# A two-level Strassen matmul with tanh on one core: s3 made first in a tile of its own, the opening's stores moved, two products of chunk 0 made plain, 24 zero matmuls ahead

## The chip, the cores and the metric

The kernel runs on one core of one Trainium2 chip. The metric is the device time of one launch in microseconds (us). The time before is 1428.15 us, the median of three runs (1426.63, 1428.15 and 1431.34). A single profiled execution of the same kernel took 1431.41 us; its span in the trace is 1429.1 us.

## The reference

```python
m, k, n = 4096, 4096, 4096
# a: [4096, 4096] fp32, b: [4096, 4096] fp32, bias: [4096] fp32
return np.tanh(np.matmul(a, b) + bias)
```

Inputs and output are fp32 in DRAM. The kernel casts a and b to fp16 while loading them, multiplies in fp16 and adds in fp32.

## The kernel before

**Two levels of Strassen.** A straight matmul would need 8192 steps of 128x128 by 128x512 on TensorE (PE). The kernel uses the Winograd form of Strassen's algorithm instead. A *pair* is 256 rows of a; its four quarters are a11, a12 (the first 128 rows, low and high half of k) and a21, a22 (the other 128 rows). VectorE (DVE) forms

- s1 = a21 + a22, s3 = a11 - a21, s2 = s1 - a11, s4 = a12 - s2 from a,
- t1 to t4 in the same way from b,

and seven products of half size take the place of eight: P1 (a11), P2 (a12), P3 (s4), P4 (a22), P5 (s1), P6 (s2), P7 (s3), each against a quarter of b or a t. A *duo* is two pairs. Over a duo most products are *fine*: a second level of the same scheme is laid over the two pairs, so that one product becomes 7 groups of 8 matmuls of 128x256, from sums of the operands of the two pairs (xs3, ys3, zs3 from the two s3's, for instance). A *plain* product takes the two pairs separately, as 2 x 16 matmuls of 128x512. Fine products are `fine_product` (L852) and, in the middle part of the program, L1590; plain ones are `product` (L836).

**Stages.** The columns of b are cut into four chunks of 1024. There are 16 pairs, so 8 duos. The trace shows:

- 0 to about 95 us, the *opening*: 18 matmuls on a tile of zeros (`WARM`, L20, issued at L1986), then the first rows of a come in through transposes on PE (tile `first`, L2106) and through DVE's stream transposes (tile `land`, L510), into tiles o00 to o71; some rows are multiplied with b directly (L2067).
- about 95 to 401 us, the rest of chunk 0, duo by duo (L836, L852). While PE works on one duo, GpSimd (POOL) loads the rows of the next one into `nat` tiles (L534, four DMAs of 128 KB each, cast to fp16), DVE transposes them (L510) and makes the sums (L477).
- about 401 to 1075 us, chunks 1 and 2 together, all fine at 128x512 (L1590).
- about 1075 to 1429 us, chunk 3, all fine at 128x256: pass one (P1, P2, P6 of all duos) and pass two (P7, P5, P4, P3 of all duos, from about 1230 us).

**What sets the order.** The program records each step as an operation with its reads and writes; a planner then simulates engines and DMA (with the constants `RATES`, `SHARES`, `WARM_TIME`, `NAT_LEAD`, `SLACK_OPEN`) and writes down one fixed order for each engine, and one of 51 places in SBUF for each tile. SyncE (SP) issues every store and every load from scratch memory in DRAM, in that order; POOL issues the loads of a and b. ScalarE (ACT) copies to and from PSUM (L480) and does the tanh.

**Names the change touches.** `natural` (L559) loads and sums one pair: with `own=True` (first duo after the opening only) s3 gets a tile of its own first and s1 too; otherwise s1 gets the tile of its own, and s3 is written over a21 once s1 has read a21. `over=True` (the middle duos) leaves s2 to later (`natural_late`), where s2 is written over a11. The opening's two pairs, 0 and 1, do the same with `half_sum` (L2206 to L2208). `keep` stores sums in scratch memory (L598) for the later chunks; `KEEP_AT` says for each of the two opening pairs whether its stores come with its sums (0) or later (1). `STEEP` counts, for each duo of chunk 0 behind the opening's, how many of its products are fine: the first x of P1, P7, P5 (L2282); the others are plain. `TOGETHER` says how many of a chunk's last duos go product by product in place of duo by duo. `BEHIND` is the number of P1's that stand ahead of the first P2 in a pass, `AFTER` a position in the same order.

Of the kernel before, what the change touches and what calls it, by code (L numbers as in the profile page):

```python
# [16 lines left out]
TB = 4  # L17
TP = T // 2
G = 2
WARM = 18  # L20
fp32 = mybir.dt.float32
fp16 = mybir.dt.float16
pair32 = mybir.dt.uint32
ADD = mybir.AluOpType.add
SUB = mybir.AluOpType.subtract
# [9 lines left out]
LASTING = ((), (), (), ())  # L35
SHARED = True
SOFT = 1.5
BEHIND = 2
FARTHER = (50, 65, 40, 50)
THREE = (False, True, True, True)  # L40
AFTER = (6, 6, 6, 7)
HOLD = (1, 1, 1, 3)
KEEP_AT = (0, 1)
NAT_LEAD = 2.0
FIRST = (0, 1)
CLASSIC = 16
LATE_STORES = 2
SLACK_OPEN = 0.8
WHOLE = ()
SPARE = ("a11", "a12", "a22")  # L50
AHEAD = ((), (), (), (), (), ())
# [6 lines left out]
RING = 8  # L58
SPEED, SLACK = 1.0, 0.8
RATES = (  # L60
    {"POOL": (378e3, 3.7), "LONG": (419e3, 3.7), "in": (354e3, 4.1), "out": (377e3, 3.9)},
    {"POOL": (386e3, 3.6), "LONG": (399e3, 3.6), "in": (376e3, 3.4), "out": (380e3, 3.6)},
    {"POOL": (375e3, 3.9), "LONG": (403e3, 3.9), "in": (396e3, 3.4), "out": (395e3, 3.5)},
)
SHARES = (
    ((0.29, 0.49, 0.37), (0.40, 0.53, 0.57)),
    ((0.39, 0.45, 0.47), (0.44, 0.55, 0.58)),
    ((0.32, 0.40, 0.45), (0.47, 0.55, 0.54)),
)
FIRST_AT = 1.4  # L70
WARM_TIME = 6.7
RISE = ((), (4, 4, 4, 4, 4, 4, 4, 4), (4, 4, 4, 4, 4, 4, 4, 4), (4, 4, 4, 4, 4, 4, 4, 4))
SECONDS = (0, 8, 8, 8)
STEEP = ((0, 1, 2, 2, 2, 3), (), ())
BASIS = ("a11", "a12", "a22", "s2")
STORED = BASIS + ("s1", "s3", "s4")
LEFT = ('P6', 'P7', 'P5', 'P4', 'P3')
Q_ORDER = (0, 2, 1, 3)
WIDE = 1
WIDE_LASTING = ('s3', 's1')  # L80
TOGETHER = (0, 0, 0, 0)
WIDE_ORDER = (7, 6, 1, 5, 4, 3, 2, 0)
WIDE_PASSES = ((("P1", 0),), (("P2", 0),), (("P6", 0), ("P7", 1)), (("P4", 0),), (("P5", 0), ("P3", 1)))
TURN = 5
WIDE_EARLY = {'P1': (11.0, 80), 'P2': (11.0, 90), 'P6': (11.0, 100), 'P7': (8.0, 120), 'P4': (11.0, 70), 'P5': (11.0, 50), 'P3': (18.0, 100)}


class Buf:
# [324 lines left out]
def kernel(  # L413
# [142 lines left out]

                add("DVE", turn_time(1024), emit, (tl,), (s[name],), soft=soft)

    def natural(pair, kept, own=False, spare=(), over=False):  # L559
        s = {}  # L560
        for r in range(2):
            natural_rows(pair, r, s)
        if own:
            asum(s, "s3", "a11", "a21", SUB)
        asum(s, "s1", "a21", "a22", ADD)
        if over:
            if kept:
                keep(pair, s, BASIS[:2], spare=spare, soft=3.0)
            asum(s, "s3", "a11", "a21", SUB, over="a21")
            return s  # L570
        asum(s, "s2", "s1", "a11", SUB)
        if not own:
            asum(s, "s3", "a11", "a21", SUB, over="a21")
        if kept:
            keep(pair, s, spare=spare)
        return s
# [25 lines left out]
    def keep(pair, s, names=BASIS, spare=(), after=None, soft=None):  # L602

        for name in names:
            soft = soft or (3.0 if names is BASIS else 12.0)
            if pair % 2 == 0:
                move(name, pair // 2, 1, s[name], 0, 2, True, soft=soft, after=after)
                continue
            move(name, pair // 2, 3, s[name], 1, 1, True, soft=soft, after=after)
            if name not in spare:  # L610
                move(name, pair // 2, 4, s[name], 0, 1, True, soft=soft, after=after)
# [1350 lines left out]
    early = set(range(4, NP)) | set(FIRST)  # L1962
# [197 lines left out]
    d = first_duo  # L2160
# [8 lines left out]
    behind = None  # L2169
    if LATE_STORES:  # L2170
# [3 lines left out]
        behind = plan.ops[-1]  # L2174
# [12 lines left out]
    def half_sum(s, name, x, y, op, over=None, halves=(0, 1)):  # L2187
        x, y = s[x], s[y]
        if name not in s:
            s[name] = s[over] if over else new(name, [P, T, P], atoms=2)  # L2190

        def atoms(v, h):
            return (h,) if len(v.atoms) == 2 else (2 * h, 2 * h + 1)

        for h in halves:
            key = ALL, ds(h * TP, TP)
            tt(
                at(s[name], *key), at(x, *key), at(y, *key), op, TP * P,
                ((x, atoms(x, h)), (y, atoms(y, h))), ((s[name], atoms(s[name], h)),), wide=False,
            )  # L2200
# [5 lines left out]
    d.a, d.last_sum = [], last_sum  # L2206
    for p in FIRST:
        s = {f"a{r + 1}{h + 1}": aq[2 * p + r, h] for r in range(2) for h in range(2)}  # L2208
        half_sum(s, "s1", "a21", "a22", ADD)
        half_sum(s, "s3", "a11", "a21", SUB, over="a21")  # L2210
        half_sum(s, "s2", "s1", "a11", SUB)
        firsts[p] = s
        d.a.append(s)
        if not KEEP_AT[p]:
            keep(p, s, [n for n in BASIS if n != "a22" or p != LATE_STORES - 1], soft=3.0)
    d.c, d.k, d.bop, d.pairs = 0, k0, bop, list(FIRST)
    d.x, d.next, d.put = 0, STEEP[0][0], ()
    d.parts = d.last = d.stays = False
# [5 lines left out]
    for c in range(NC):  # L2224
        duos = [[2 * i, 2 * i + 1] for i in ORDER[c]]
        if c in (WIDE, WIDE + 1):
            if c == WIDE:
                plan.open = 2
                if before:
                    waiting.append(lambda between, before=before: (before(), between()))  # L2230
                wide_pass(c, held)
                before = held = None
                for s in sets:
                    for bank in s:
                        ring.remove(bank.index // 2)
                        ring.append(bank.index // 2)
                whole.update(p for p in range(NP) if held_names.get(p, set()) >= set(HELD))
            continue
        if c >= TWO:
            plan.open = 2  # L2240
            k = load_bias(c)
            finish_bias(k)
            bop, rights = {}, {}
            for name in ("b11", "b21"):
                for blk in range(4):
                    raw_b(bop, c, name, blk, NEAR)
            rights["P1"] = fine_right(bop, "b11", True, NEAR)
            if SECONDS[c]:
                rights["P2"] = fine_right(bop, "b21", True, NEAR)
            if before:  # L2250
                waiting.append(lambda between, before=before: (before(), between()))

            def rest():
                for blk in range(4):
                    for name in ("b12", "b22"):
                        raw_b(bop, c, name, blk, (NEAR, FARTHER[c]))
                    bsums(bop, blk, (NEAR, FARTHER[c]))

            if THREE[c]:
                rest()  # L2260
                rights["P6"] = fine_right(bop, "t2", True, NEAR)
            on_chip = pass_one(c, k, bop, rights, duos, held)
            if not THREE[c]:
                rest()
            pass_two(c, k, bop, rights, duos[::-1], on_chip)
            before = held = None
            continue
        fines = {}
        for i, pairs in enumerate(duos):
            d = Duo()  # L2270
            d.c, d.k, d.bop, d.pairs = c, k, bop, sorted(pairs)
            d.parts = c > 0 and i == 0
            d.last = d.stays = i == len(duos) - 1 and c < TWO - 1
            d.x = STEEP[c][i]
            d.next = (STEEP[c] + (0,))[i + 1]
            duo = d.pairs[0] // 2
            over = OVER and 0 < i < len(duos) - 1
            d.a = [natural(p, p in early, i == 0, SPARE if p % 2 and duo not in WHOLE else (), over) for p in d.pairs]
            for name in BASIS if i == 0 else () if over else BASIS[1:]:
                sigma(name, duo, d.a)  # L2280
            if d.x and not d.parts:
                for name, r in (("P1", "b11"), ("P7", "t3"), ("P5", "t1"))[:d.x]:  # L2282
                    if name not in fines:
                        fines[name] = fine_right(bop, r)
            d.right = fines
            d.put = AHEAD[i]
            for name in d.put:
                if name != "s4":
                    for s in range(2):
                        put_by(d, name, s)  # L2290
# [55 lines left out]
```

## Time and profile before

| what | value |
|---|---|
| time, median of 3 (all) | 1428.15 us (1426.63, 1428.15, 1431.34) |
| the profiled execution: its own time, its span | 1431.41 us, 1429.1 us |
| PE | 1417.6 us busy (99%), 8386 matmuls |
| DVE | 1090.6 us busy (76%) |
| ACT | 395.6 us busy (28%) |
| POOL | 325.4 us busy (23%) |
| mean granted TensorE clock | 0.998 |
| DMA | 399.19 MB, 279 GB/s on average |

All times are from one profiled execution, and those of a place in the program are counted from the start of its span. "Busy" for PE counts matmuls whose ends are modelled and overlap, so the time of a run of matmuls is best taken from the start of its first to the start of what follows. In a timeline row stand the start, the duration of the group, the engine, the line and the operation, `out<-in`, shape and count; in brackets the idle time ahead of it and what ended it. In a windows row stand the stretch, its length, PE's or DVE's busy time and instructions in it, the granted clock (1.00 is full, 0.50 half), the busy share of the 16 DMA engines and GB/s.

### The profile page before, as it was taken

What the parts mean: (1) busy time and instruction counts of PE and PEld (TensorE: products, weight loads), DVE (VectorE), ACT (ScalarE), POOL (GpSimd) and SP (SyncE); (2) the same over time, 40 slices, a digit from 0 to 9 for tenths busy, and PEclk for the clock granted to TensorE, in tenths of its full rate; (3) what the DMA queues carried; (4) which work ended last, traced back from release to release, by engine and by line L of the source; (5) the groups of instructions that cost most, each with busy time, mean ns of one, the idle gap of its engine ahead of it and who ended that gap; (6) DMA issues with size and microseconds to landing.
All of it is one profiled execution on the core that took longest, in us unless ns stands there. A gap on an engine that the chain in (4) does not pass through costs nothing.

```text
span 1429.1 us, 22558 instructions
## 1 busy us (share of the span) xinstructions
PE 1417.6 (99%) x8386; PEld 820.4 (57%) x8386; DVE 1090.6 (76%) x1617; ACT 395.6 (28%) x752; POOL 325.4 (23%) x613
## 2 busy tenths in 40 slices
PE   8999999999999999999999999999999999999998
PEld 3444555555644444444444444444447888888887
DVE  3679878767985476795568787988797689997876
ACT  3121212222233333311111233233323332243433
POOL 8764432334452331100111130000130400000000
PEclk9999999999999999999999999999999999999999
DMA  9999998899999899997889799999999987788883
GB/s 177 180 224 291 278 293 208 216 250 210 284 274 315 235 272 307 280 375 273 270 283 299 264 309 380 338 362 354 332 333 347 281 246 260 251 295 291 314 291 134
DMA packets 167485, 399.19 MB, mean 279 GB/s; under 512 B 25424, under 2 KB 44368, under 8 KB 167376
## 3 DMA queue, kind: packets, MB, share of 16 engines
q1 hardware_dynamic: 104400, 318.03, 61.4%
q0 software_dynamic: 62976, 79.73, 33.6%
q8 instruction: 66, 1.08, 0.3%
q14 instruction: 43, 0.35, 0.1%
HBM read 327.68 MB, written 149.68 MB: 334 GB/s over the span
## 4 chain that ended last, share of the span: by engine, by line
PE 78%; DMA 1%; DVE 1%; ACT 0%; issue 0%; SPq 0%; DVEq 0%
PE ps L1590 47%; PE ps L852 25%; PE ps L836 6%; DMA xa<-a 1%; DVE parts L477 0%; ACT parts L1388 0%; DVE za L688 0%; DVE s L477 0%; DVE a L477 0%; DVE ps L477 0%; DVE t L477 0%; DVE cs L477 0%; DVE a L510 0%; ACT ps L480 0%; SPq L491 0%
## 5 line engine op out<-in xcount | busy, mean ns | idle before, releaser
L763 POOL DMA_DIRECT2D b<-in_b_dram x320 | 169.8, 535 | 608.9 <-DMA out_dram<-u 165.4
L480 ACT COPY ps<-ps 128x512 f32<-128x512 f32 (+1 forms) x218 | 101.9, 468 | 445.7 <-PE ps L1590 308.9
L534 POOL DMA_DIRECT2D nat<-in_a_dram x224 | 118.5, 533 | 204.7 <-DMA nat<-in_a_dram 47.3
L477 DVE TENSOR_TENSOR parts<-ps,parts 128x256 f32<-128x256 f32 (+1 forms) x131 | 73.8, 564 | 75.0 <-PE ps L1590 39.6
L477 DVE TENSOR_TENSOR u<-ps,u 128x512 f32<-128x512 f32 x160 | 106.1, 685 | 28.2 <-PE ps L1590 27.4
L836 PEld LDWEIGHTS <-a 128*128 128x128 f16 x768 | 75.1, 98 | 86.9 <-DVE a L477 0.2
L477 DVE TENSOR_TENSOR ps<-ps,parts 128x256 f32<-128x256 f32 (+1 forms) x155 | 85.2, 555 | 38.7 <-PE ps L1590 23.0
L480 ACT COPY parts<-ps 128x256 f32<-128x256 f32 (+1 forms) x153 | 70.1, 463 | 135.8 <-DVE ps L477 45.2
L1590 PE MATMUL ps<-b,zs 128*128 128x512 f16 x448 | 105.8, 379 | 0.0
L1590 PEld LDWEIGHTS <-ya 128*128 128x128 f16 x624 | 61.0, 98 | 73.6
L836 PE MATMUL ps<-b,a 128*128 128x512 f16 x448 | 99.1, 379 | 0.0
L510 DVE STREAM_TRANSPOSE a<-nat 128x512 uint32<-128x512 uint32 x112 | 73.1, 689 | 21.1 <-DMA nat<-in_a_dram 15.2
L2067 PE MATMUL ps<-b,o 128*128 128x512 f16 x384 | 84.9, 384 | 0.0
L1590 PEld LDWEIGHTS <-zs 128*128 128x128 f16 x512 | 50.1, 98 | 60.2
L1590 PEld LDWEIGHTS <-xa 128*128 128x128 f16 x512 | 50.1, 98 | 60.2
L477 DVE TENSOR_TENSOR b<-b,b 128x2048 f16<-128x2048 f16 (+2 forms) x76 | 68.2, 909 | 12.6 <-DMA b<-in_b_dram 10.1
L1590 PE MATMUL ps<-b,za 128*128 128x512 f16 x320 | 75.6, 379 | 0.0
L836 PE MATMUL ps<-t,a 128*128 128x512 f16 x320 | 72.3, 379 | 0.0
L498 ACT ACTIVATE parts<-ps 128x512 f32<-128x512 f32 x50 | 29.7, 596 | 145.6 <-PE ps L836 97.2
L2067 PEld LDWEIGHTS <-o 128*128 128x128 f16 x384 | 37.8, 99 | 45.6 <-issue 1.1
L1590 PEld LDWEIGHTS <-za 128*128 128x128 f16 x384 | 37.6, 98 | 45.3
L852 PEld LDWEIGHTS <-ya 128*128 128x128 f16 x592 | 57.9, 98 | 7.1
(177 smaller groups left out, 2586.3 us busy)
## 6 DMA issues: line engine op xcount, KB each, us to landing
b<-in_b_dram POOLq DMA_DIRECT2D x320, 128.0 KB, 7.9
ya<-a SPq DMA_DIRECT2D x70, 512.0 KB, 6.8
xa<-a SPq DMA_DIRECT2D x70, 512.0 KB, 6.7
u<-U SPq DMA_DIRECT2D x62, 512.0 KB, 6.9
nat<-in_a_dram POOLq DMA_DIRECT2D x224, 128.0 KB, 7.8
U<-u SPq DMA_DIRECT2D x48, 512.0 KB, 7.0
ys<-s SPq DMA_DIRECT2D x46, 512.0 KB, 4.9
xs<-s SPq DMA_DIRECT2D x46, 512.0 KB, 5.4
```

Source lines behind the costliest of these rows:

```text
L477: dve(n, lambda: nc.vector.tensor_tensor(out=o(), in0=x(), in1=y(), op=op), reads, writes, wide, **kw)
L480: act(n, lambda: nc.scalar.copy(o(), x()), reads, writes, **kw)
L498: act(NB, lambda: nc.scalar.activation(o[ALL], src[ALL], TANH), (src,), (o,), soft=2.0)
L510: nc.vector.transpose(dst[ALL].rearrange("P t m -> P (t m)").bitcast(pair32).rearrange("P (U m) -> P U m", m=P)[:, ds(t0 // 2, nu), ds(row ...
L534: nc.gpsimd.dma_start(out=tl[(ds(q * QP, QP), *key)], in_=src)
L763: nc.gpsimd.dma_start(out=dst.rearrange("p t j n -> p t (j n)") if j is None else dst, in_=src)
L836: nc.tensor.matmul(bank[ALL], left_tile(left, k + t + shift), rb.tile(t), start=start and k == t0 and t == 0, stop=k + t == t0 + nt - 1, s ...
L852: nc.tensor.matmul(bank[ALL, HALF[half]], left_tile(buf, at_ * TP + i * TB + t), rb.tile(t), start=False, stop=i == 1 and t == TB - 1, ski ...
L1590: nc.tensor.matmul(bank[ALL, cols], left_tile(buf, at_ * TP + i * TB + t), rb.tile(t, half), start=start and not (i or t), stop=i == 1 and ...
L2067: nc.tensor.matmul(bank[ALL], left_tile(left, t), rb.tile(tb), start=start, stop=stop, skip_group_check=True,)
```

## The change

The diff, cut to what has an effect that the prediction speaks of:

```diff
-WARM = 18
+WARM = 24
-BEHIND = 2
+BEHIND = 3
-AFTER = (6, 6, 6, 7)
+AFTER = (6, 6, 6, 5)
-KEEP_AT = (0, 1)
+KEEP_AT = (0, 0)
-NAT_LEAD = 2.0
+NAT_LEAD = 1.0
-SLACK_OPEN = 0.8
+SLACK_OPEN = 1.0
-WARM_TIME = 6.7
+WARM_TIME = 7.6
-STEEP = ((0, 1, 2, 2, 2, 3), (), ())
+STEEP = ((0, 1, 2, 2, 2, 2), (), ())
-TOGETHER = (0, 0, 0, 0)
+TOGETHER = (0, 0, 0, 3)
...
-    def natural(pair, kept, own=False, spare=(), over=False):
+    def natural(pair, kept, spare=(), over=False):
...
-        if own:
-            asum(s, "s3", "a11", "a21", SUB)
-        asum(s, "s1", "a21", "a22", ADD)
+        asum(s, "s3", "a11", "a21", SUB)
+        asum(s, "s1", "a21", "a22", ADD, over="a21")
         if over:
             if kept:
                 keep(pair, s, BASIS[:2], spare=spare, soft=3.0)
-            asum(s, "s3", "a11", "a21", SUB, over="a21")
             return s
         asum(s, "s2", "s1", "a11", SUB)
-        if not own:
-            asum(s, "s3", "a11", "a21", SUB, over="a21")
...
-        half_sum(s, "s1", "a21", "a22", ADD)
-        half_sum(s, "s3", "a11", "a21", SUB, over="a21")
+        half_sum(s, "s3", "a11", "a21", SUB)
+        half_sum(s, "s1", "a21", "a22", ADD, over="a21")
...
-            keep(p, s, [n for n in BASIS if n != "a22" or p != LATE_STORES - 1], soft=3.0)
+            keep(p, s, [n for n in BASIS if n != "a22" or p != LATE_STORES - 1], after=behind, soft=3.0)
```

Besides, numbers of the planner's model of DMA (`RATES`, `SHARES`) and of how early it loads (`FARTHER`, and for chunks 1 and 2 `WIDE_EARLY`) are changed, which moves single steps of DVE, ACT and SP past one another and gives tiles other places in SBUF. By `STEEP`, P5 of the last duo of chunk 0 is fine before and plain after. PE has 8368 matmuls after in place of 8386: six more of zeros, 56 of 128x256 fewer and 32 of 128x512 more. DVE has 15 sums fewer, ACT 10 copies fewer; POOL's and SP's numbers of DMAs stay (608 and 725).

**DVE, the rows ahead of the fourth duo's P7 in chunk 0 (269 to 280 us in the trace before).** The names are tiles; a number behind a name tells one pair's tile from another's. First before:

```order
L510 STREAM_TRANSPOSE a22_2452<-nat_2359 128x2x8x32
L510 STREAM_TRANSPOSE a21_2461<-nat_2359 128x2x8x32
L477 TENSOR_TENSOR s1_2491<-a21_2461,a22_2452 128x2048
L477 TENSOR_TENSOR a21_2461<-a11_2258,a21_2461 128x2048
L477 TENSOR_TENSOR ys3_2504<-a21_2461 128x1024
L510 STREAM_TRANSPOSE a22_2471<-nat_2415 128x2x8x32
L510 STREAM_TRANSPOSE a21_2474<-nat_2415 128x2x8x32
L477 TENSOR_TENSOR s1_2517<-a21_2474,a22_2471 128x2048
L477 TENSOR_TENSOR a21_2474<-a11_2269,a21_2474 128x2048
L477 TENSOR_TENSOR ys3_2504<-ys3_2504,a21_2474 128x1024
```

and after:

```order
L510 STREAM_TRANSPOSE a21_2478<-nat_2385 128x2x8x32
L477 TENSOR_TENSOR s3_2497<-a11_2274,a21_2478 128x2048
L477 TENSOR_TENSOR ys3_2504<-s3_2497 128x1024
L510 STREAM_TRANSPOSE a22_2510<-nat_2342 128x2x8x32
L510 STREAM_TRANSPOSE a21_2481<-nat_2433 128x2x8x32
L477 TENSOR_TENSOR s3_2523<-a11_2296,a21_2481 128x2048
L477 TENSOR_TENSOR ys3_2504<-ys3_2504,s3_2523 128x1024
L477 TENSOR_TENSOR zs3_2535<-s3_2523,s3_2497 128x1024
L477 TENSOR_TENSOR zs3_2535<-s3_2523,ys3_2504 128x1024
L510 STREAM_TRANSPOSE a22_2510<-nat_2433 128x2x8x32
L477 TENSOR_TENSOR a21_2481<-a21_2481,a22_2510 128x2048
```

Before, each pair's s1 stands between the transposes and its s3 (the row `a21 <- a11, a21`); after, s3 stands directly behind the transpose of a21, and the last a22 and s1 (the row `a21 <- a21, a22`) come behind all that P7 needs.

**PE, the last duo of chunk 0, around the start of P5 (about 381 us before).** Before:

```order
L836 LDWEIGHTS s2_3433
L836 MATMUL ps_1_239<-t2_861,s2_3433 128x512
L852 LDWEIGHTS s1_3375
L852 MATMUL ps_6_273<-t1_1111,s1_3375 128x256
L852 LDWEIGHTS s1_3375
```

and after:

```order
L832 LDWEIGHTS s2_3453
L832 MATMUL ps_1_245<-t2_867,s2_3453 128x512
L832 LDWEIGHTS a21_3293
L832 MATMUL ps_4_267<-t1_1154,a21_3293 128x512
L832 LDWEIGHTS a21_3293
```

Behind the last matmul of P6 (s2 against t2) stands P5 (s1 against t1): before in groups of 128x256, after at 128x512 from s1 in a21's place. The plain P5 is 32 matmuls in place of 56.

**SP, its first rows behind the load of the bias (97 to about 131 us before).** a_0_68 to a_0_70 and s_0_71 are the scratch for a11, a12, a22 and s2 of the first duo, out_dram is the output. Before:

```order
L598 DMA a_0_68<-o_224 128x2048
L598 DMA a_0_69<-o_402 128x2048
L598 DMA a_0_70<-o_404 128x2048
L598 DMA s_0_71<-s_760 128x2048
L491 DMA out_dram<-parts 128x512 x2
L598 DMA a_0_70<-o_417 128x1024 x2
L598 DMA a_2_82<-a_1044 128x2048
L491 DMA out_dram<-parts 128x512
L598 DMA a_2_83<-a_1068 128x2048
L491 DMA out_dram<-parts 128x512 x12
```

and after:

```order
L491 DMA out_dram<-parts 128x512
L594 DMA a_0_70<-o_423 128x1024 x2
L491 DMA out_dram<-parts 128x512
L594 DMA a_2_82<-a_1051 128x2048
L491 DMA out_dram<-parts 128x512 x8
L594 DMA a_0_68<-o_230 128x2048
L594 DMA a_0_69<-o_408 128x2048
L594 DMA a_0_70<-o_410 128x2048
L594 DMA a_0_68<-o_255 128x1024 x2
L594 DMA a_0_69<-o_414 128x1024 x2
L491 DMA out_dram<-parts 128x512 x4
```

The stores of pair 0 move from ahead of all output stores to behind ten of them, and pair 1's a11 and a12 (o_249 and o_408 before, o_255 and o_414 after, two DMAs each) come directly behind them; before they were row 29 and 30 of SP's list, in the trace at 160.72 us.

In chunk 3, `BEHIND` and `AFTER` put each P2 of pass one one duo later, and `TOGETHER` has the last three duos of pass two run P7, P7, P7, P5, P5, P5, P4, P4, P4, P3, P3, P3 in place of P7, P5, P4, P3 three times.

More of the change, by code (lines that the diff above doesn't have):

```diff
@@ L37 @@
 SOFT = 1.5
-BEHIND = 2
-FARTHER = (50, 65, 40, 50)
+BEHIND = 3
+FARTHER = (50, 65, 40, 45)
 THREE = (False, True, True, True)
-AFTER = (6, 6, 6, 7)
+AFTER = (6, 6, 6, 5)
 HOLD = (1, 1, 1, 3)
-KEEP_AT = (0, 1)
-NAT_LEAD = 2.0
+KEEP_AT = (0, 0)
+NAT_LEAD = 1.0
 FIRST = (0, 1)
@@ L60 @@
 RATES = (
-    {"POOL": (378e3, 3.7), "LONG": (419e3, 3.7), "in": (354e3, 4.1), "out": (377e3, 3.9)},
-    {"POOL": (386e3, 3.6), "LONG": (399e3, 3.6), "in": (376e3, 3.4), "out": (380e3, 3.6)},
-    {"POOL": (375e3, 3.9), "LONG": (403e3, 3.9), "in": (396e3, 3.4), "out": (395e3, 3.5)},
+    {"POOL": (379e3, 3.5), "LONG": (421e3, 3.5), "in": (354e3, 4.1), "out": (371e3, 3.5)},
+    {"POOL": (395e3, 4.1), "LONG": (402e3, 4.1), "in": (400e3, 3.2), "out": (380e3, 3.4)},
+    {"POOL": (391e3, 4.1), "LONG": (403e3, 4.1), "in": (390e3, 3.3), "out": (390e3, 3.35)},
 )
 SHARES = (
-    ((0.29, 0.49, 0.37), (0.40, 0.53, 0.57)),
-    ((0.39, 0.45, 0.47), (0.44, 0.55, 0.58)),
-    ((0.32, 0.40, 0.45), (0.47, 0.55, 0.54)),
+    ((0.30, 0.48, 0.46), (0.36, 0.61, 0.55)),
+    ((0.38, 0.46, 0.55), (0.50, 0.555, 0.607)),
+    ((0.32, 0.37, 0.48), (0.475, 0.53, 0.54)),
 )
 FIRST_AT = 1.4
-WARM_TIME = 6.7
+WARM_TIME = 7.6
 RISE = ((), (4, 4, 4, 4, 4, 4, 4, 4), (4, 4, 4, 4, 4, 4, 4, 4), (4, 4, 4, 4, 4, 4, 4, 4))
 SECONDS = (0, 8, 8, 8)
-STEEP = ((0, 1, 2, 2, 2, 3), (), ())
+STEEP = ((0, 1, 2, 2, 2, 2), (), ())
 BASIS = ("a11", "a12", "a22", "s2")
@@ L84 @@
 TURN = 5
-WIDE_EARLY = {'P1': (11.0, 80), 'P2': (11.0, 90), 'P6': (11.0, 100), 'P7': (8.0, 120), 'P4': (11.0, 70), 'P5': (11.0, 50), 'P3': (18.0, 100)}
+WIDE_EARLY = {'P1': (11.0, 90), 'P2': (11.0, 90), 'P6': (11.0, 100), 'P7': (8.0, 120), 'P4': (11.0, 70), 'P5': (8.0, 50), 'P3': (11.0, 90)}
 class Buf:
@@ L2277 @@
             over = OVER and 0 < i < len(duos) - 1
-            d.a = [natural(p, p in early, i == 0, SPARE if p % 2 and duo not in WHOLE else (), over) for p in d.pairs]
+            d.a = [natural(p, p in early, SPARE if p % 2 and duo not in WHOLE else (), over) for p in d.pairs]
             for name in BASIS if i == 0 else () if over else BASIS[1:]:
```

## The prediction

> **What bounds the kernel now.** The first thing to read is the head of the page.
>
> ```profile
> span 1429.1 us, 22558 instructions
> PE 1417.6 (99%) x8386; PEld 820.4 (57%) x8386; DVE 1090.6 (76%) x1617; ACT 395.6 (28%) x752; POOL 325.4 (23%) x613
> ```
>
> PE is busy for 1417.6 of 1429.1 us, so 11.5 us is all that waits, head and tail can hold. A change here either changes PE's work or these 11.5 us. The second view is PE's waits (engine, line, what it waited for: us in all, times, the longest).
>
> ```profile
> PE ps L852 <- DVE a L477: 2.8, 1, 2.8
> PE tp L2106 <- DMA first<-in_a_dram: 2.7, 1, 2.7
> PE warm L1986 <- DVE zeros L1980: 1.4, 1, 1.4
> PE ps L852 <- DVE ps L477: 0.3, 1, 0.3
> PE ps L852 <- ACT ps L480: 0.2, 1, 0.2
> ```
>
> Five waits, 7.4 us; the other 4 us are head and tail around the program. The third is the chain that ended last (start, us, engine, line, count).
>
> ```profile
> 406.63 668.22 PE ps L1590 x3096
> 1138.36 284.03 PE ps L852 x2600
> ```
>
> From 406 us to the end PE works nearly without a gap, 668.22 / 3096 = 0.2158 us for a matmul of 128x512 and 284.03 / 2600 = 0.1092 us for one of 128x256. So chunks 1 to 3 can hardly win; they can only lose. The gains have to be in the first 280 us, and there are three places: the two waits above, and the granted clock, which the windows show (stretch, length, PE busy and matmuls, clock, DMA share, GB/s):
>
> ```profile
> 4.20:7.60 3.40, 2.86 (x16) 1.00 1.04 150
> 7.60:11.05 3.45, 1.27 (x12) 1.00 1.50 185
> 11.05:14.46 3.41, 3.41 (x13) 0.50 1.28 186
> ```
>
> Behind a stretch in which PE was busy 1.27 of 3.45 us the clock is half for 3.41 us. At full clock this work takes half the time, so the half clock costs about 1.7 us. It stands in no row of waits.
>
> **The change part by part.** Terms are against the profiled execution's own 1431.41 us.
>
> *s3 first.* The 2.8 us wait is this (PE, then POOL's last load for that duo, then DVE):
>
> ```profile
> 264.92 10.52 PE L836 MATMUL ps<-b,a 128*128 128x512 f16 x48
> 278.24 1.05 PE L852 MATMUL ps<-b,a 128*128 128x256 f16 x8 [2.80 <-DVE a L477]
> ...
> 263.59 2.24 POOL L534 DMA_DIRECT2D nat<-in_a_dram  x4 [1.06 <-PE ps L836]
> nat<-in_a_dram POOLq DMA_DIRECT2D x224, 128.0 KB, 7.8
> ...
> 269.76 1.30 DVE L510 STREAM_TRANSPOSE a<-nat 128x512 uint32<-128x512 uint32 x2 [3.16 <-DMA nat<-in_a_dram]
> 271.10 1.23 DVE L477 TENSOR_TENSOR s<-a,a 128x2048 f16<-128x2048 f16 x1
> 272.36 1.23 DVE L477 TENSOR_TENSOR a<-a,a 128x2048 f16<-128x2048 f16 x1
> 273.69 0.69 DVE L477 TENSOR_TENSOR ys<-a 128x1024 f16<-128x1024 f16 x1
> 274.30 1.30 DVE L510 STREAM_TRANSPOSE a<-nat 128x512 uint32<-128x512 uint32 x2
> 275.69 1.23 DVE L477 TENSOR_TENSOR s<-a,a 128x2048 f16<-128x2048 f16 x1
> 276.95 1.23 DVE L477 TENSOR_TENSOR a<-a,a 128x2048 f16<-128x2048 f16 x1
> ```
>
> PE is ready at 264.92 + 10.52 = 275.44 and starts at 278.24, when the second s3 (the row at 276.95) is done. DVE had started on the duo's last rows at 269.76, and two transposes of a22 (0.65 each) and two s1 (1.23 each), 3.76 us, stood among what P7 needs. In the new order one a22 transpose stays, so 1.23 + 1.23 + 0.65 = 3.1 us leave. That only helps if the rows have landed: the last of the four DMAs starts at about 265.3, and 7.8 us later is 273.1 (an estimate; DVE's transpose at 274.30 is the upper bound). Transpose of a21 and s3 then end at 273.1 + 0.65 + 1.23 = 275.0, at most 276.2. So P7 starts between 0 and 0.8 us late. What is late next is s2, which P6 reads. How long P7 covers it the last duo shows, where nothing waits:
>
> ```profile
> 371.80 1.04 PE L852 MATMUL ps<-b,a 128*128 128x256 f16 x8
> 376.17 3.62 PE L836 MATMUL ps<-t,s 128*128 128x512 f16 x16
> ```
>
> P6 follows P7's start by 4.37 us, here at 279.8. Behind s3 DVE has three sums of 0.69 (ys, zs, zs), the a22 transpose 0.65, s1 1.23, one more of 0.69 and s2 1.23, so s2 ends near 275.0 + 5.6 = 280.6: 0.8 us late, or not, if the loads come earlier. I take half, 0.4. Term: -2.8 + 0.4 = **-2.4** (from -2.8 to -1.6; 0 if the duo's loads come later by as much).
>
> *24 zeros.* PE's rows in the opening:
>
> ```profile
> 6.67 0.39 PE L2106 MATMUL tp<-ident,first 128*128 128x128 f16 x4
> 9.78 0.41 PE L2106 MATMUL tp<-ident,first 128*128 128x128 f16 x4 [2.72 <-DMA first<-in_a_dram]
> ```
>
> Six more zeros are 6 x 0.2158 = 1.3 us; they push the four transposes from 6.67 to 7.97 and end well ahead of 9.78, where a DMA ends the wait: they cost nothing, the wait shrinks instead. If the data of 9.78 came 1.4 us earlier in a run, that cover would be gone, and they would cost 1.3. What they change is the clock: 7.60 to 11.05 would be busy for 1.27 + 1.3 = 2.6 us, near the 2.86 of the stretch before, behind which the clock stayed, and far from 1.27, behind which it fell. Term: **-1.7** (from -1.7 to 0).
>
> [...]
>
> *P5 plain in chunk 0's last duo.* 56 x 0.1092 = 6.12 us become 32 x 0.2158 = 6.91: **+0.8**. DVE and ACT lose 15 and 10 operations, on engines that PE doesn't wait for there: nothing. That P5 reads s1 from a21's place: s1 is made before P6, nothing.
>
> *The opening's stores.* The same bytes on the same queue; SP's waits are nobody's but the readers' of `parts` and of places that come free. Pair 1's four DMAs of 256 KB stand here:
>
> ```profile
> 160.72 4.02 SPq L598 DMA_DIRECT2D a<-o  x4
> 130.00:157.00 27.00, 27.00 (x127) 1.00 1.08 306
> ```
>
> They move to about 115 to 135 us, into a stretch where the DMA engines are full (the second row): at most 1 MB / 306 GB/s = 3.4 us for other transfers, bought back behind 160. I take 0, since the second duo has 1.7 us to spare (below).
>
> *Chunk 3.* `BEHIND`, `AFTER`, `TOGETHER` and the planner's numbers move order, not work. The two small waits, 0.3 + 0.2, lie in pass one; they may go or come again elsewhere: **-0.2** (from -0.5 to +0.5).
>
> Sum: -2.4 - 1.7 + 0.8 - 0.2 = -3.5, so 1431.41 - 3.5 = 1427.9. The profiled execution is 3.3 us above the median of the runs, 1428.15. The three runs spread over 4.7 us, about as much as the clock's drop and the wait at 278 together, and both hang on when a DMA lands; so part of what I subtract will not have been in the median run. If all of the 3.3 is the profile's own, the result is 1424.6; if none is, 1427.9. I take the middle: **1426.3**.
>
> **The rivals.**
>
> - *Only half of it happens.* The clock falls all the same (+1.7), or s2 or the loads are later (+0.8 to 1.6): 1427.1 to 1428.6. [...] Against: 2.6 us busy is near 2.86.
> - *More goes.* All of the gap is the profile's, both small waits go too and P6 doesn't wait: 1424.6 - 0.4 - 0.3 = 1423.9, and down to 1423 if the wait on `first` gets shorter. For it: the three terms are independent of one another. Against: the fastest of three runs is 1426.63, and with +0.8 of work it can hardly fall by 3.
> - *The stores delay the second duo.* PE reaches that duo's P1 here, behind DVE's last transpose of a11 and two zs:
>
> ```profile
> 158.39 0.70 DVE L510 STREAM_TRANSPOSE a<-nat 128x512 uint32<-128x512 uint32 x1
> 160.76 1.04 PE L852 MATMUL ps<-b,a 128*128 128x256 f16 x8
> ```
>
>   The transpose ends at 159.1, 1.7 us ahead, and PE comes 1.7 earlier if the clock stays full. With nothing to spare, 3.4 us of DMA ahead of the `nat` loads would be lost whole: 1426.3 + 3.4 = 1429.7. Against: SP's queue before held pair 0's stores ahead of these loads too, and they now come later.
> - *Slower: DVE in pass two.* With the last three duos together, three P7, three P5, three P4 and three P3 follow each other. DVE in the duo before the last, by product's length:
>
> ```profile
> 1363.50:1369.60 6.10, 3.77 (x7) 1.00 0.71 222
> 1369.60:1375.80 6.20, 6.20 (x9) 1.00 0.90 332
> 1375.80:1381.90 6.10, 6.03 (x10) 1.00 0.94 320
> ```
>
>   Of a duo's four stretches two are full (6.2 and 6.0) and two half empty; now duo by duo a full one is followed by an easy one, and after three full ones come together. If in each of six such stretches one sum of 0.69 no longer fits, PE waits 6 x 0.69 = 4.1 us: 1430.4; with two sums, 8.3 us: 1434.6. It ends slower than before from about 0.7 + 0.3 us a stretch on: 6 x 1.02 = 6.1 takes 1426.3 to 1432.4. For it: DVE's rows show no spare there. Against: the sums of one product need not stay in its stretch, and the easy stretches (3.77) come in threes as well, so buffers can be filled ahead.
>
> **How the numbers follow.** About what a measurement can tell from no change is 0.3%, 4.3 us: faster is below 1423.9, slower above 1432.4. Forecast 1426.3 (1424.6 to 1427.9): 0.50. Half of it: 0.17. More goes: 0.12, taken as below 1423.9. Stores: 0.09. DVE in pass two: 0.10, half of it with one sum (1430.4), half with two (1434.6). Something unforeseen in the moved planner orders, slower: 0.02. So faster 0.12; slower 0.05 + 0.02, and 0.02 of the stores' case if waits chain, 0.09; the same 0.79. The range 1423.7 to 1430.6 takes in the forecast, the half, the stores and one sum, 0.81 + a little of "more goes".
>
> **What would show it.** In the profile after: no wait of PE at P7 of the fourth duo (about 270 to 276 us), or one of under 0.8 us, and perhaps a new one at its P6; the granted clock 1.00 in all windows behind 4.2 us; 24 zeros ending near 8 us and a wait on `first` of about 1.4 us in place of 2.7; PE's busy time 1417.6 + 1.3 + 0.8 - 1.7 = 1418.0; the plain P5 with 32 matmuls of 0.2158 ahead of chunk 1. The stores' case would show as a wait on DVE or `nat` near 159 us, DVE's case as rows of waits on DVE between 1350 and 1425 us. The forecast is wrong if PE's waits in the profile after add up to over 5 us, or if the time moves though they don't.

## The result, and the profile after

The changed kernel is slower. Over 20 runs each its median is 1432.53 us (1430.07 to 1436.58), that of the kernel before 1429.64 us (1426.63 to 1433.19): a ratio of 1.0020, with a 95% interval of 1.0011 to 1.0028, or 2.9 us. Run once more (e5 below) it stood at 1.0033 (1.0020 to 1.0046). The forecast was 1426.3 us, the range 1423.7 to 1430.6; the time lies above it.

The head of the page and PE's waits of the changed kernel's profiled execution (1434.56 us, span 1432.8):

```profile
span 1432.8 us, 22489 instructions
PE 1419.2 (99%) x8368; PEld 817.0 (57%) x8368; DVE 1083.0 (76%) x1602; ACT 390.8 (27%) x742; POOL 325.6 (23%) x613
```

```profile
PE ps L848 <- DVE ps L477: 1.7, 1, 1.7
PE warm L1982 <- DVE zeros L1976: 1.4, 1, 1.4
PE ps L848 <- DVE s L477: 1.4, 1, 1.4
PE tp L2102 <- DMA first<-in_a_dram: 1.0, 1, 1.0
PE ps L1586 <- ACT ps L480: 0.9, 1, 0.9
PE ps L848 <- ACT ps L480: 0.7, 1, 0.7
PE ps L832 <- DVE parts L477: 0.4, 1, 0.4
PE ps L832 <- DVE a L477: 0.3, 1, 0.3
PE ps L832 <- DVE s L477: 0.3, 1, 0.3
```

The 2.8 us at P7 and much of the wait on `first` are gone, and seven waits have come that were not there; one of them, at P6 of the fourth duo, was forecast. Where they stand, from start to start of PE's matmuls, so that the sums close (us, after less before):

| place | before | after | difference |
|---|---|---|---|
| opening, with the six zeros and the half clock | 6.1 | 3.2 + 1.3 | -1.6 |
| P7 of the third and fourth duo and the P6 behind it (231, 275 us) | 3.2 | 0.5 | -2.7 |
| P7 and P6 of the fifth duo (320 to 328 us) | 0 | 2.7 | +2.7 |
| P7 to P3 of the sixth duo (374 to 393 us) | 0 | 2.9 | +2.9 |
| near 562 us, in chunks 1 and 2 | 0 | 1.1 | +1.1 |
| pass one of chunk 3 | 0.9 | 0.3 | -0.6 |
| P5 of the sixth duo (from 384.8 us before, 385.5 after), matmuls alone | 6.1 | 6.9 | +0.8 |
| PE's last matmul to the end of the span | 4.1 | 5.3 | +1.2 |

The sum is +3.8, the spans differ by 1432.8 - 1429.1 = 3.7.

At the fourth duo the step went as worked out: P7 starts without a wait, and what is late next is s2, by 0.3 us (PE's rows):

```profile
276.89 1.04 PE L848 MATMUL ps<-b,s 128*128 128x256 f16 x8
278.22 3.63 PE L832 MATMUL ps<-t,a 128*128 128x512 f16 x16 [0.29 <-DVE a L477]
```

In the sixth duo, the last of chunk 0, PE's rows and DVE's beside them:

```profile
373.60 1.04 PE L848 MATMUL ps<-b,s 128*128 128x256 f16 x8
374.92 3.63 PE L832 MATMUL ps<-t,s 128*128 128x512 f16 x16 [0.28 <-DVE s L477]
380.27 1.03 PE L848 MATMUL ps<-f4t,s 128*128 128x256 f16 x8 [1.72 <-DVE ps L477]
```

```profile
374.78 1.30 DVE L510 STREAM_TRANSPOSE a<-nat 128x512 uint32<-128x512 uint32 x2
376.11 1.23 DVE L477 TENSOR_TENSOR a<-a,a 128x2048 f16<-128x2048 f16 x1
377.44 1.23 DVE L477 TENSOR_TENSOR s<-a,a 128x2048 f16<-128x2048 f16 x1
378.58 0.69 DVE L477 TENSOR_TENSOR parts<-a 128x1024 f16<-128x1024 f16 x1
379.19 0.68 DVE L477 TENSOR_TENSOR parts<-s 128x1024 f16<-128x1024 f16 x1
379.79 0.76 DVE L477 TENSOR_TENSOR ps<-ps,parts 128x256 f32<-128x256 f32 x2
```

PE starts the 16 matmuls of P6 as soon as the first s2 is done, and they cover 3.45 us. DVE needs 5.0 us from there (374.78 to 379.79) for the other pair's a22, s1 and s2 and two sums `parts`, and only then comes the sum in PSUM that frees the bank for PE's next group. The wait is about that difference and the sum's own 0.4. The two sums `parts` are 1.2 us of it; without them some 0.7 would be left (an estimate from these rows). The same wait, 1.88 us from start to start, stands in the second profile of this kernel. In the profile before, with the fine P5 and s1 ahead of s3, the same sum starts 1.7 us ahead of PE's group, which does not wait (DVE, then PE):

```profile
377.96 0.75 DVE L477 TENSOR_TENSOR ps<-ps,parts 128x256 f32<-128x256 f32 x2
379.62 1.04 PE L852 MATMUL ps<-f4t,a 128*128 128x256 f16 x8
```

In the fifth duo, PE's rows and ACT's:

```profile
322.15 1.05 PE L848 MATMUL ps<-b,s 128*128 128x256 f16 x8 [1.37 <-DVE s L477]
...
325.66 1.03 PE L848 MATMUL ps<-f2t,ys 128*128 128x256 f16 x8 [0.71 <-ACT ps L480]
```

```profile
324.73 0.60 ACT L498 ACTIVATE parts<-ps 128x512 f32<-128x512 f32 x1 [6.77 <-DVE a L510]
325.23 0.38 ACT L480 COPY ps<-ps 128x256 f32<-128x256 f32 x1
```

PE waits for a copy of 0.38 us on ACT that stands behind a tanh, and by the profile the tanh waited for one of DVE's transposes of a22.

At the end, SP's last rows and the instruction queue in the last 7.5 us:

```profile
1426.31 2.30 SPq L1516 DMA_DIRECT2D out_dram<-cs  x2
1428.71 0.38 SPq L1224 DMA_DIRECT2D out_dram<-cs  x1
1429.18 0.91 SPq L1516 DMA_DIRECT2D out_dram<-cs  x2
```

```profile
q8 instruction: 1, 0.02, 1.1%
```

Two stores take 2.30 us (before: 0.81 and 1.19 for two pairs of them), while a packet of 16 KB of instructions arrives. Slow stores are not the whole of a longer end, though: in the second profile of this kernel (e5) it is 6.1 us, and the pairs of stores take 0.81 and 1.19 us there.

### The profile page after: what moved, and what is told of

It reads as the page before. It is cut to its first block, busy times and chain, and to the rows that moved or that the text cites. A ratio compares the mean times of both kernels' runs of the same rounds, so it can differ in the third digit from the quotient of the medians.

```text
span 1432.8 us, 22489 instructions
## 1 busy us (share of the span) xinstructions
PE 1419.2 (99%) x8368; PEld 817.0 (57%) x8368; DVE 1083.0 (76%) x1602; ACT 390.8 (27%) x742; POOL 325.6 (23%) x613
## 4 chain that ended last, share of the span: by engine, by line
PE 81%; DMA 11%; DVE 5%; issue 2%; POOL 1%; ACT 0%; SPq 0%; DVEq 0%; POOLq 0%
PE ps L1586 47%; PE ps L848 23%; DMA nat<-in_a_dram 6%; PE ps L2063 6%; PE ps L832 5%; DMA a<-parts 2%; DVE a L477 1%; DVE parts L477 1%; DVE a L510 1%; DMA s<-a 1%; DMA xa<-a 1%; DVE s L477 1%; DVE ps L477 0%; DMA first<-in_a_dram 0%; POOL nat L534 0%
## 5 line engine op out<-in xcount | busy, mean ns | idle before, releaser
L832 PEld LDWEIGHTS <-a 128*128 128x128 f16 x928 | 90.5, 98 | 107.7 <-DVE a L477 1.0
L832 PE MATMUL ps<-t,a 128*128 128x512 f16 x512 | 114.0, 379 | 0.4 <-DVE a L477 0.3
L832 PE MATMUL ps<-b,a 128*128 128x512 f16 x416 | 92.1, 379 | 0.4 <-DVE parts L477 0.4
```

The lines of the kernel that those rows point to most:

```text
L832: nc.tensor.matmul(bank[ALL], left_tile(left, k + t + shift), rb.tile(t), start=start and k == t0 and t == 0, stop=k + t == t0 + nt - 1, s ...
```

## The experiments

Each kernel is compared with runs of the kernel before on the same chip. `B` stands for the kernel before, `A` for the changed one. "Waits from start to start" are worked out from the starts of neighbouring matmuls; about 0.16 us more than the profile's waits.

**e1 to e4: one part alone on B.** e1:

```diff
-WARM = 18
+WARM = 24
```

> The kernel before with 24 zeros in place of 18 and every engine's order otherwise unchanged. All theories: the granted clock stays full behind 4.2 us, and PE reaches the second duo about 1.6 us earlier (1.7 of clock and 1.3 of wait less, 1.3 of zeros more). Theory G (given back): the rows of a land when they land, so the wait at the fourth duo's P7 grows from 2.8 to about 4.4 us and the time is that of before within 0.5 us. Rival O (new order on DVE) and rival N (planner's numbers): the gain stays, the wait stays at 2.8 us, the time is about 1.6 us below before.

Ratio 1.0001 (0.9987 to 1.0015). The wait at the fourth duo's P7 is 3.3 us, neither 4.4 nor 2.8, and the clock didn't do what all theories said: it fell to half, but behind that wait. The windows around it (stretch, length, PE busy, clock, DMA share, GB/s):

```profile
273.13:276.55 3.42, 0.80 (x4) 1.00 0.52 202
276.55:279.96 3.41, 2.76 (x14) 0.50 0.80 157
279.96:283.37 3.41, 3.41 (x31) 1.00 0.96 264
```

So e1's wait at P7 cost more than itself. e3, with the same order there, shows a half clock behind it too (0.61 on average over 276.20 to 279.70 us, 0.89 over the 3.30 us after); B's own profile has it in the opening instead (0.50 from 11.05 to 14.46 us).

e2, `natural` and the opening's sums as in the change:

```diff
-        asum(s, "s1", "a21", "a22", ADD)
+        asum(s, "s3", "a11", "a21", SUB)
+        asum(s, "s1", "a21", "a22", ADD, over="a21")
```

> The kernel before with s3 made first in a tile of its own and s1 in a21's place, nothing else by hand. G: the wait at the fourth duo's P7 (2.8 us) goes, and waits for rows of a at the fifth and sixth duo's P7 or P6 come back with 2 to 2.8 us in all; the time is that of before within 0.7 us. O: waits on DVE at P6 and P5 of the fifth and sixth duo of 3 to 5 us in all, whose cause is s1 and a22 behind s3, though the rows of a have landed in time; the time is 1 to 3 us above before. N: 2.4 us below before.

Ratio 0.9987 (0.9976 to 0.9998), 1.9 us below B by the ratio: between G and N, and of all versions the only one whose interval lies below B. The wait at the fourth duo is gone, nothing waits at the fifth duo's P7 or P6, and about 3 us of small waits stand elsewhere: 1.4 us at 230 to 237, 0.7 at 376 to 395, and 1.0 at the entrance to chunks 1 and 2 (405 to 409). Part of the gain is given back, though not where G said. The 1.9 us hang on the chip too: the kernel before has a median of 1430.67 us there and of 1428.70 on the chip of e15 and e16, two later kernels with s3 first, while e2, e15 and e16 themselves lie within 0.6 us of one another (1428.98, 1428.56, 1429.12).

e3:

```diff
-BEHIND = 2
+BEHIND = 3
-AFTER = (6, 6, 6, 7)
+AFTER = (6, 6, 6, 5)
-TOGETHER = (0, 0, 0, 0)
+TOGETHER = (0, 0, 0, 3)
```

> The kernel before with chunk 3's order alone (BEHIND, AFTER, TOGETHER). If the stores that come together at the end hold up the last ones: the stretch from PE's last matmul to the end of the span grows by about 1 us, the time is 1 us above before. If the longer end of the profile after was chance: within 0.3 us of before. No wait of PE over 0.5 us in pass two by either.

1.0005 (0.9994 to 1.0017), no difference shown. The end of the span is 4.1 us, as before: the last stores' bunching is not the cause. Pass two has no wait over 0.1 us that the kernel before does not have; pass one has one of 1.6 us near 1127.

e4, `RATES`, `SHARES`, `FARTHER`, `NAT_LEAD`, `SLACK_OPEN`, `WARM_TIME` and `WIDE_EARLY` alone:

> The kernel before with the planner's numbers alone (RATES, SHARES, FARTHER, NAT_LEAD, SLACK_OPEN, WARM_TIME, WIDE_EARLY). N: new waits of PE in chunk 0's last two duos and one near 562 us, 2 to 4 us in all, the time that much above before. G and O: at most the wait near 562 us (0 to 1.1 us), the wait at the fourth duo's P7 as before, the time within 1 us of before.

0.9993 (0.9980 to 1.0007). Of N's waits only one of 0.4 us near 555 us came, and the wait at the fourth duo's P7 went by itself (0.2 us left), because POOL starts the duo's last load near 262 us in place of 265. N falls as far as the numbers alone are meant: no single one of these four parts makes the loss.

**e5 to e8: A again, and A with one part undone.** e5 is A unedited.

> The changed kernel once more, unedited, for a second profile beside the first. If its waits belong to its order: again 4 to 6 us of PE's waits at P7 to P3 of chunk 0's fifth and sixth duo (320 to 395 us), about 1 us near 562 us, and 5 us from PE's last matmul to the end of the span in place of 4. If they were chance: other places and sums. The time is 1431.5 to 1433.5 us either way.

1433.7 us, 1.0033. The waits belong to the order: 0.87, 0.30 and 1.88 us from start to start at 323, 325 and 376 us are the same to a hundredth in both profiles; those that wait for rows of a (1.4 at 320, 0.4 at 392) are not there or smaller. Between 320 and 395 us that leaves 3.3 us of waits in place of 5.6, under the 4 to 6 that were expected, and the end of the span is 6.1 us, over the 5. The wait near 562 us is 2.1 in place of 0.9, and costs more than that. PE's windows, then ACT's, DVE's and PE's rows there:

```profile
558.97:562.39 3.42, 1.31 (x7) 1.00 0.57 177
562.39:565.81 3.42, 3.42 (x10) 0.50 0.92 368
565.81:569.20 3.39, 3.39 (x17) 1.00 0.84 290
```

```profile
559.38 2.00 ACT L1879 ACTIVATE o<-o 128x1024 f32<-128x1024 f32 x2 [7.09 <-issue]
561.29 0.58 ACT L480 COPY ps<-ps 128x512 f32<-128x512 f32 x1
...
556.88 1.23 DVE L477 TENSOR_TENSOR b<-b,b 128x2048 f16<-128x2048 f16 x1 [6.69 <-DMA b<-in_b_dram]
558.02 1.88 DVE L477 TENSOR_TENSOR o<-ps,u 128x512 f32<-128x512 f32 x3
...
561.92 3.15 PE L1586 MATMUL ps<-b,a 128*128 128x512 f16 x8 [2.11 <-ACT ps L480]
```

DVE stands at a sum of b whose rows have not landed; the sums `o` behind it are late, so ACT's tanh of `o` is late, and the copy that PE needs stands behind the tanh. That the tanh waits for these sums is read from the tiles' names and times; the profile itself names nothing that it waited for.

e6 is A with the planner's numbers of B:

> The changed kernel with the planner's numbers of before (RATES, SHARES, FARTHER, NAT_LEAD, SLACK_OPEN, WARM_TIME, WIDE_EARLY). Theory N2 (with these numbers the sixth duo's rows are asked for later, at 327 us in place of 320, and PE then waits for sums): the waits between 320 and 395 us fall to under 2 us and the one near 562 goes, the time is 3 to 5 us below the changed kernel. Rival D (s1 and a22 behind s3 make the waits, whatever the numbers): the waits stay, 4 to 6 us, the time is that of the changed kernel within 1 us.

1.0005 (0.9996 to 1.0014), 1429.4 us in place of e5's 1433.7. No wait over 0.2 us between 148 and 1124 us. In the sixth duo the sum that PE waited for is early, although more stands ahead of it, because the last rows landed earlier: POOL starts the duo's last load at 351.5 us, in A at 358.0 (DVE, then PE):

```profile
371.93 1.22 DVE L477 TENSOR_TENSOR a<-a,s 128x2048 f16<-128x2048 f16 x1
373.07 0.76 DVE L477 TENSOR_TENSOR ps<-ps,parts 128x256 f32<-128x256 f32 x2
...
375.08 1.04 PE L848 MATMUL ps<-f4t,s 128*128 128x256 f16 x8
```

N2 holds and D falls, as they were put; e9 and e10 then show that the numbers do not do it alone.

e7 is A with chunk 3's order of B (e3's edit backwards):

> The changed kernel with chunk 3's order of before (BEHIND, AFTER, TOGETHER). If the three P3's together hold up the last stores: the stretch behind PE's last matmul is 4 us in place of 5, the time 1 us below the changed kernel. By every other theory: within 0.5 us of it.

1.0014 (1.0003 to 1.0024). The end is 5.4 us: not chunk 3's order. The waits of chunk 0 are as in e5 and more. The time, 1430.9 us, is all the same 2.8 below e5's on the same chip, where the theories gave 1 us at most; against the first 20 runs it is 0.9 below by the ratios. Whether chunk 3's order costs something in A stays open.

e8 is A with the stores of the opening where they were:

> The changed kernel with the opening's stores where they were (KEEP_AT, after). Theory K (the stores push the fifth and sixth duo's loads back, or take their places in SBUF): waits between 320 and 395 us under 2 us, the time 3 us below the changed kernel. N2 and D: waits stay, time within 1 us of it.

1.0017 (1.0004 to 1.0030). Its one profile has only 0.7 us of waits between 320 and 395 us, all of it where A has its 1.88, which speaks for K, while the time, 1432.5 us, does not fall by 3 us. Left open: one profile and the median disagree here. The profiled execution took 1429.64 us, 2.8 below the median of its kernel, so it need not show what the others waited for.

**e9 to e12.** e9 is A with a fine P5:

```diff
-STEEP = ((0, 1, 2, 2, 2, 2), (), ())
+STEEP = ((0, 1, 2, 2, 2, 3), (), ())
```

> The changed kernel with P5 of chunk 0's last duo fine again (STEEP 3). Theory O2 (the plain P5 puts two sums of 0.69 ahead of the answer that PE waits 1.9 us for near 378 us, and costs 0.8 us of matmuls): that wait falls to 0.5 to 0.8 us, PE's work by 0.8 us, the time is 1.5 to 2.2 us below the changed kernel. If the wait comes from late rows of a: it stays at 1.9 us, the time is 0.8 below. If from the planner's numbers alone: as this last.

0.9993 (0.9982 to 1.0003), 1429.2 us: more than was expected, 4.5 us below e5 and 3.4 below the first median, which were not measured beside it (by the ratios to the kernel before 5.7 and 3.9). The wait near 378 is gone altogether; the sum stands directly behind s2 now (DVE, then PE), and the fifth duo's 0.87 and 0.31 stay:

```profile
373.57 1.23 DVE L477 TENSOR_TENSOR s<-a,a 128x2048 f16<-128x2048 f16 x1
374.72 0.76 DVE L477 TENSOR_TENSOR ps<-ps,parts 128x256 f32<-128x256 f32 x2
...
376.19 1.04 PE L848 MATMUL ps<-f4t,s 128*128 128x256 f16 x8
```

Two things have moved here. The two sums of 1.2 us stand behind the answer now; and the last s2 starts 0.8 us behind P6's start (373.57 against 372.73) in place of 2.5 (377.44 against 374.92), since its loads moved too: POOL starts the duo's last one at 355.1 us in place of 358.0. So e9 shows what the plain P5 costs in A's order, not what the two sums alone cost.

e10 is A with s1 before s3, as in B:

> The changed kernel with s1 before s3 as it was (natural and the opening's pairs). Rival D (s1 and a22 behind s3 make the waits at 322 to 328 and 372 to 380 us): these go, the wait of 2.8 us at the fourth duo's P7 is back, the time is that of the changed kernel within 1.5 us. N2 (the numbers make them): waits between 320 and 395 us stay at 3 us or more, and the one at the fourth duo's P7 comes on top: 1 to 3 us above the changed kernel.

1.0017 (1.0005 to 1.0029), 1432.3 us. The waits from 320 to 395 are all gone, as D said, and the one at P7 is back (the second row; the first is the one near 560 us):

```profile
PE ps L1590 <- ACT ps L480: 1.8, 1, 1.8
PE ps L852 <- DVE a L477: 1.6, 1, 1.6
```

The time hardly falls, since the wait at P7 has come in place of the others. So in these profiles the sixth duo's wait takes three things at once: s1 and s2 behind s3, a plain P5 with its two sums ahead, and rows that land later by the new numbers. Taking out any one removes it (e6, e9, e10). With the opening's stores taken back 0.7 of it is left (e8), so they may be a fourth.

e11 is B with s3 first and the new numbers:

> The kernel before with s3 first and with the planner's numbers, no other edit. If numbers and s3 first together make the waits (each alone did not): 2 to 4 us of PE's waits between 320 and 395 us and the one near 562, the time 1 to 3 us above before. If plain P5 or the stores are needed for it: under 1 us of waits there, the time 1.5 to 3 us below before.

0.9994 (0.9982 to 1.0007). Waits of 2.0 us between 320 and 396 (0.87 and 0.30 among them, not the 1.88), of 1.4 near 560, of 0.8 near 110 and of 0.9 near 407, and yet no loss against B, whose own wait at P7 is gone: in between the two expectations.

e12 is e6 with a fine P5:

> A version meant to beat both: the changed kernel with the planner's numbers of before and P5 of chunk 0's last duo fine (so s3 first, the stores, 24 zeros and chunk 3's order remain). If the numbers made the waits and the plain P5 costs its 0.8 us: no wait over 0.5 us between 230 and 400 us, and the time 1 to 2 us below before. If s3 first is good for nothing without them: that of before within 0.7 us.

0.9996 (0.9986 to 1.0006). It does not beat B: new waits of 0.9 us at the entrance to chunks 1 and 2 and of 2.1 in pass one, where chunk 3's order with the old numbers has its wait in e3 and e6 too.

**e13 to e16: what was still open.** e13 is B with a plain P5:

> The kernel before with P5 of chunk 0's last duo plain (STEEP 2) and nothing else by hand. Theory P (the plain P5 is the main cost of the change): 0.8 us of matmuls, 1 to 2 us more from PE's last matmul to the end of the span (the last 16 KB of PE's instructions arrive among the last stores), and a wait for sums behind P6 near 380 us of up to 2 us; the time 2 to 4 us above before. Rival Q (it costs only with the planner's new numbers): 0.8 to 1.5 us above before.

1.0009 (0.9998 to 1.0021), 1.2 us above B, no wait near 380, an end of 4.1 us. Q fits: alone, the plain P5 costs about its 0.8, in an interval from a little below nothing to 3 us.

e14 is A with more zeros of a small shape:

```diff
+        for i in range(18):
+            nc.tensor.matmul(ps[ALL, :64], zeros[ALL, :P], zeros[ALL, :64], start=i == 0, stop=i == 17)
```

> The changed kernel with 18 more matmuls of zeros of 128x64 behind the 24 (0.5 us of work in a wait of 1 us), so that PE's stream is 36 instructions longer. If the longer end comes from the place of the last fetch of PE's instructions: that fetch starts about 2 us earlier and the end is 4.1 us in place of 5.3 and 6.1, the time about 1.2 us below the changed kernel. If it comes from the order of the last stores: 5.3 us again, the same time within 0.5 us.

The trace does as the first theory said: the last fetch starts 3.5 us ahead of PE's last matmul in place of 0.6, the end is 4.2 us, and the two stores take 0.81 again:

```profile
1426.85 0.81 SPq L1516 DMA_DIRECT2D out_dram<-cs  x2
```

The time does not: 1434.07 us, 1.0040 (1.0026 to 1.0054), not below A. Its profile has more waits in chunk 0 than A's (7.3 us from 320 to 394 in place of 5.6). So the end's 1.2 us are shown in the spans of profiles, not in the median time.

e15 is e2 with the stores of the change, e16 is e2 with 24 zeros:

> A version meant to beat both: the kernel before with s3 first and with the opening's stores behind the last rows, everything else as before. If the stores cost nothing: 1.5 to 3 us below before, as s3 first alone. If they hold up the second duo's rows: a wait near 160 us of 1 us or more and the time within 1 us of before.

> A version meant to beat both: the kernel before with s3 first and 24 zeros. If zeros matter for the clock in the opening: no run with a lower mean clock than 1.0 and the time 0.3 us or more below that of s3 first alone (1.9 us below before). If only the wait at the fourth duo's P7 matters: the same clocks and time as with 18 zeros, within 0.5 us.

e15: 0.9994 (0.9983 to 1.0006), no wait near 160 us, so the stores cost nothing there. e16: 1.0002 (0.9991 to 1.0014), with two of 12 runs below a mean clock of 1.0, against e2's one of 12: no sign that the zeros keep the clock. In both, PE arrives earlier at chunks 1 and 2 and waits there, in e15:

```profile
PE ps L1586 <- DMA b<-in_b_dram: 0.7, 1, 0.7
```

## Why the prediction was wrong

*"P5 plain ... 6.12 us become 6.91: +0.8. DVE and ACT lose 15 and 10 operations, on engines that PE doesn't wait for there: nothing."* This is the step that failed. The matmuls are right; the rest is not nothing. With the change of P5 two sums stand ahead of the one that PE needs behind P6, and with the rows' landing in A that is a wait of 1.88 us, of which the two sums themselves are 1.2; taking the plain P5 back (e9) lowers the median by 3.4 (first 20 runs) to 4.5 us (e5), where 0.8 was counted; with the order of before its cost fits the 0.8 (e13). The working counted how many operations DVE lost, not which ones stand ahead of the one that PE waits for.

*"`BEHIND`, `AFTER`, `TOGETHER` and the planner's numbers move order, not work ... -0.2."* The second failure. The numbers cost waits near 562 us (0.4 to 2.3 us from start to start in all nine profiles of kernels that have them, none in the nine of those that do not, B among them), and in the fifth duo 0.8 to 0.9 + 0.3 in six of the seven profiles that have s3 first as well. Taking them back (e6) brings the time to 1.0005 of the kernel before. The bound of +0.5 was taken from two waits of before, although a new order can bring a wait at any place that had room before.

*"Chunks 1 to 3 can hardly win ...; they can only lose."* Right, and the forecast gave them 0.10 for DVE in pass two, which did not come, and 0.02 for "something unforeseen in the moved planner orders, slower", which did.

*s3 first, -2.4.* The mechanism is right, wait and next wait (0.3, against the 0.4 taken). The gain is not kept: e2, e15 and e16 end 1.9 and 0.9 us below B and 0.3 above it, and all three wait at 403 to 410 us, where B doesn't. In A's own order as much is lost again at each of two places, the fifth duo (2.7 us) and the sixth (2.9), where s1 and s2 come later too.

*24 zeros, -1.7.* Between the two profiles it came out as worked out: no drop of the clock, and 1.6 us less in the opening. That was luck, since it hung on the one profile that it was taken from. The drop in the opening is in B's profile only; none of the six other profiles with 18 zeros has it (their mean clock is 1.0 in five; in e3 it is 0.999, with the half clock behind P7). PE starts its 381st matmul behind the zeros at 90.8 us there, at 88.8 to 89.8 in those six, and at 89.1 to 89.7 in the eleven profiles with 24 zeros or more: without the drop the zeros show no gain. Nor did e1's 24 zeros make a full clock more frequent: 3 of its 12 runs have a mean of 1.0, B on the same chip 9 of 35. What goes with a full clock is s3 first: 106 of 142 runs of the kernels with it are at 1.0, 27 of 60 of the edited ones without it. A mean of 0.999 says little, because the half clock behind PE's last matmul alone makes it in the profiles of A (0.72 from 1430.00 to 1432.80 us, where no matmul stands, and 1.00 ahead of that), e8 and e10; but a mean of 0.998 or less, which that alone makes in no profile, stands in 6 of the 142, in 8 of the 60 and in 28 of 131 runs of B. The wait at P7 behind which the clock fell in e1 and e3 is gone with s3 first; that this is the reason is likely, not shown. A term of 0, the other end of its range, fits these runs better than the -1.7.

*The middle between the profile's own time and the median.* It rested on three runs with a median of 1428.15; 20 runs put B at 1429.64, so 1.5 us of the miss stand in the starting point. Part of B's spread goes with the mean granted clock: runs at 1.0 average 1428.4 us (60 runs), the others 1430.9 (71). A at 1.0 averages 1432.4 us (18 runs of both sets), so among the runs at 1.0 A loses 4.0 us. A part of that is hidden, since its clock falls less often (0.998 or less in 2 of 29 runs, B's in 28 of 131).

*The rivals.* DVE's pass two did not come (no wait of over 0.1 us there in A or e3 that B does not have); the stores did not (no wait near 160 us in A or e15). The mechanism of the slower rival, a full DVE whose answer PE waits for, is what came, in chunk 0 and not in chunk 3. The sign that the prediction named for itself came too: PE's waits in the profile after add up to 8.1 us, over 5.

*Two figures of the working.* The 5.6 us up to s2 hold from start to start only (the durations that are listed add up to 5.9), and 1428.6 is no sum of the steps that it stands for (1426.3 + 1.7 + 0.8 = 1428.8). Neither bears on the outcome.

## What to carry to other kernels

Where a planner writes the order, an edit's price is not the work it removes or adds: read, for each wait of the engine that bounds the time, which rows of the other engines' new order stand ahead of the answer, and do so at every place that had little room before. A wait taken away early can show up again at the next place that depends on a load's landing, as at 403 to 410 us in e2, e15 and e16 (on rows of b 0.3, 0.7 and 0.3 us). Judge parts together: three edits, none of which shows a loss of its own beyond noise, made a wait of 1.9 us that is gone from the profile when any one of them is undone.

## What the hardware showed unexpectedly

**Two waits of B of nearly the same length, one with a half clock behind it.** Behind B's wait of 2.72 us on `first` the granted clock is 0.50 for 3.41 us, from 11.05 us on. In that stretch its matmuls of 128x512 start 0.43 us apart, behind it 0.22. The stretch ahead had PE busy for 1.27 of 3.45 us. Ahead of the half clock in e1 it was busy for 0.80 of 3.42 us, in e5 for 1.31 of 3.42, in e3, ahead of the row of 0.61, for 0.60 of 3.20; in e1 and e5 the clock is 1.00 again after 3.41 and 3.42 us. The half clock cost B about 1.7 us, since PE worked all through it, and e1 about 1.4, where PE was busy for 2.76 us of it (estimates: half of 3.41 and of 2.76). B's own wait at P7, 2.80 us, cost no clock:

```profile
273.89:277.30 3.41, 1.55 (x8) 1.00 0.46 177
277.30:280.71 3.41, 2.47 (x23) 1.00 0.78 121
```

Nor did the one of 2.9 us in e13 (1.00 from 271.36 to 278.19 us, a mean of 1.0 over that run). What decides between the two is not shown.

**The last fetch of PE's instructions.** PE's stream arrives in 65 or 66 packets of 16 KB in these profiles (66 in A's and in B's). In the profiles in which the last packet's fetch starts 3.1 to 3.5 us ahead of PE's last matmul, or a 66th does not show (11 with 66 packets, three of the plain P5's with 65), the end behind PE's last matmul is 4.05 to 4.2 us. Where it starts 0.6 us ahead of it (A, at 1426.88 against 1427.53 us; e7, e8) the end is 5.3 to 5.4 us, and where 1.8 us behind it (e5) 6.1. The plain P5 makes the stream shorter (16,844 of PE's rows in A's trace, 16,883 in B's) and can so move this fetch into the last stores. It need not: e10, with as many rows as A, shows 65 packets and an end of 4.2 us. That the fetch makes the end longer rests on this agreement and on e14's one profile.
